# One 512-column product for the upper half of the expert tiles, with index numbers and gates read from PSUM

## The chip, the cores and the metric

The kernel runs on one core of a Trainium2 chip. The metric is the device time of one execution in microseconds. TensorE (PE) multiplies, with PEld as its weight loads; VectorE (DVE), ScalarE (ACT) and GpSimd (POOL) do the elementwise work; SyncE (SP) issues the transfers from HBM. SBUF is the working memory, PSUM holds the products in 8 banks of 512 float32 for each partition.

## The reference

There are two layers over 256 tokens of width 1024: a gated short convolution or an attention mixer, each followed by the same channel mixer, which is where nearly all of the time goes. Its part that matters here, for a normalised input `xc`:

```python
q = (xc @ w_q).reshape(PEER_CHUNK, PEER_HEADS, 2, PEER_HALF)
s1 = jnp.einsum('thd,nd->thn', q[:, :, 0], sub_k1); s2 = jnp.einsum('thd,nd->thn', q[:, :, 1], sub_k2)
v1, i1 = lax.top_k(s1, PEER_TOPK); v2, i2 = lax.top_k(s2, PEER_TOPK)
...
top_s, top_pos = lax.top_k(cand, PEER_TOPK)
e_idx = jnp.take_along_axis(cidx, top_pos, axis=-1)     # 16 of 16384 experts, for 8 heads
g = jax.nn.softmax(top_s, axis=-1)
a = jax.nn.gelu(jnp.einsum('td,thkd->thk', xc, u_emb[e_idx]), approximate=False)
return jnp.einsum('thk,thkd->td', g * a, v_emb[e_idx])
```

## The kernel before

The kernel gathers nothing. It multiplies the input with all 16,384 rows of `peer_u`, takes the Gelu of every product, multiplies that by a dense matrix of gates that is zero except at the chosen experts, and multiplies the result with all rows of `peer_v`. Both matrices come in 128 tiles of 128 experts for each layer: the U tiles (k = 0 to 127), then the V tiles. The products of U tile k stand in `A[:, k]`, experts in partitions and 256 tokens in columns; `A` lies in the buffer `big`.

float32 numbers are split into two float32r parts, high and low, and each product is three products: high times high, high times low, low times high. x^T stands split in `XH` and `XL`, 8 blocks of 256 columns each.

The work on one U tile goes through the engines like this, with three buffers at each stage:

- SP loads the tile into `raw` (L135). DVE transposes it to `tr` (L156). ACT copies the high part to `hi` (L170). POOL subtracts to get the low part `lo`, in two halves (L175). The last four U tiles and all V tiles have their `lo` from DVE.
- PE runs `products`: for each of 8 blocks, hi times XH (L875) and hi times XL (L876), then lo times XH for 8 blocks (L879). These are 24 matmuls of 256 columns, each with its own weight load, into half a PSUM bank. Two tiles share a bank of `lo4` (banks 0 to 3).
- After an odd tile ACT takes the Gelu of the full bank into `big` (L1011).

`next_item` is called once for each tile in program order. It emits the transpose for the tile three ahead and the split for the tile two ahead, then the tile's own products, then side work from a queue: `run_side(budget)` hands out entries as long as a credit lasts, and this order is what stands in each engine's program.

The side work of U tiles 0 to 63 is the top-k search. From U tile 64 on (`gate=U0 + 64`) it is `g_side`: for 32 groups of 8 tokens it builds the dense gates of half of the experts. For a group s, `hots` compares the numbers 0 to 63 (`iota_t`) with the group's row and column indices (`eT`) into one-hot rows in `xbuf` (DVE, L1024, 1536 elements of fp16), `gated` multiplies one part of them by the gates `gT2` (DVE, L1032, 1024 elements of fp16), PE multiplies the two for each token (16 matmuls of 64 columns, L1039, into banks 4 to 7 in turn), and `mult` multiplies `A` by the result (DVE, L1046). The second half of the experts follows in the same way beside V tiles 0 to about 58, with the banks 0 to 3; V accumulates in the other four (L483, 12 matmuls of 512 columns a tile).

Before the U tiles come the queries: `q_out` copies a query product out of PSUM, one token half on ACT (L889), the other on DVE (L890); `q_turn` has PE transpose both (L897). Between the layers, at the end of attention, `close` scales a half of the heads' outputs (DVE, L787), `fin` transposes two of their blocks and splits them (L795, L798, L799), and the output projection follows (L490 to L492).

At the end of the U tiles, `u_last` multiplies the last one; after its fourth block the side queue is emptied and `wsplit(0)` splits the first four blocks of `A` into the space of `XH` and `XL` (ACT L1066, DVE L1067) for the V tiles.

## Time and profile before

| | |
|---|---|
| median of 3 runs | 1839.16 us (1838.45 to 1839.89) |
| the profiled execution | 1836.42 us, with a span of 1834.3 us from first to last instruction |
| PE matmul busy | 1808.1 us, 99% of the span |
| DVE, ACT, POOL busy | 1340.5, 859.6, 790.5 us |
| read from HBM | 315.83 MB, 174 GB/s over the span |
| granted TensorE clock | 0.999 of full speed |

The busy time of PE is modelled for pipelined matmuls: each lasts 0.28 to 0.40 us by its row, and the next one starts before it ends. So the distance between starts is read here, not the duration. U tiles 64 to 127 of layer 0 run from 334 to 537 us of the span, those of layer 1 from 1257 to 1460 us.

### The profile page before, as it was taken

How to read it: one execution, taken by the hardware profiler on the slowest of the kernel's cores; microseconds unless marked ns; L12 is line 12 of the kernel's file. 1: busy time of each engine (PE TensorE's matmuls, PEld its weight loads, DVE VectorE, ACT ScalarE, POOL GpSimd, SP SyncE). 2: the span in 40 equal slices, each digit the busy share in tenths (PEclk: the TensorE clock that was granted, in tenths of full speed). 3: DMA queues.
4: the chain of work that ended last, by engine and by line, in shares of the span. 5: the costliest groups of instructions: out<-in, count | busy, mean ns of one | idle time of the engine just before them, and what ended most of it. 6: DMA issues, size and time to landing. Idle time of an engine off the chain costs nothing.

```text
span 1834.3 us, 34269 instructions
## 1 busy us (share of the span) xinstructions
PE 1808.1 (99%) x13009; PEld 1627.4 (89%) x13009; DVE 1340.5 (73%) x2115; ACT 859.6 (47%) x1041; POOL 790.5 (43%) x549
## 2 busy tenths in 40 slices
PE   9999999999999999999999999999999999999998
PEld 8979999999998888888788799999999988888886
DVE  4748888688778887555567587887788788875555
ACT  5455455444444444444454554555443444445443
POOL 1047899999940000000200378999999500000000
PEclk9999999999999999999999999999999999999999
DMA  6566655555555555666562565555555455556554
GB/s 210 159 197 180 183 158 172 175 170 162 167 167 173 169 177 178 226 194 194 164 185 80 179 198 171 164 165 179 167 166 166 155 181 173 173 176 227 194 194 138
DMA packets 204587, 321.26 MB, mean 175 GB/s; under 512 B 26221, under 2 KB 157317, under 8 KB 203910
## 3 DMA queue, kind: packets, MB, share of 16 engines
q1 hardware_dynamic: 202006, 312.33, 54.8%
q10 hardware_dynamic: 2416, 6.75, 1.1%
q8 instruction: 101, 1.65, 0.4%
q14 instruction: 64, 0.52, 0.1%
HBM read 315.83 MB, written 3.15 MB: 174 GB/s over the span
## 4 chain that ended last, share of the span: by engine, by line
PE 88%; DVE 4%; ACT 2%; DMA 2%; POOL 2%; issue 2%; SPq 0%; DVEq 0%; POOLq 0%; ACTq 0%
PE psum L483 40%; PE psum L875 12%; PE psum L879 12%; PE psum L876 12%; PE psum L1039 3%; PE psum L470 3%; POOL lo L175 2%; DVE big L214 1%; PE psum L516 1%; ACT hi L170 1%; DVE tr L156 1%; DVE lo L175 1%; DMA raw<-in_peer_u_dram 1%; PE psum L903 1%; PE psum L490 0%
## 5 line engine op out<-in xcount | busy, mean ns | idle before, releaser
L175 POOL TENSOR_TENSOR lo<-tr,hi 128x512 fp32r<-128x512 f32 x496 | 732.1, 1513 | 51.5 <-ACT hi L170 49.0
L175 DVE TENSOR_TENSOR lo<-raw,hi 128x1024 fp32r<-128x1024 f32 x316 | 388.2, 1229 | 257.9 <-ACT hi L170 249.3
L170 ACT ACTIVATE hi<-raw 128x1024 fp32r<-128x1024 f32 x331 | 350.1, 1060 | 450.6 <-PE psum L483 375.6
L875 PE MATMUL psum<-xh,hi 128*128 128x256 f32 x2032 | 505.2, 287 | 1.1 <-ACT hi L170 1.1
L876 PE MATMUL psum<-xl,hi 128*128 128x256 f32 x2032 | 498.4, 283 | 0.0
L483 PE MATMUL psum<-hi,xh 128*128 128x512 f32 x1104 | 435.5, 396 | 0.7 <-ACT hi L170 0.7
L483 PE MATMUL psum<-hi,xl 128*128 128x512 f32 x1104 | 428.9, 390 | 0.0
L156 DVE STREAM_TRANSPOSE tr<-raw 128x1024 f32<-128x1024 f32 x256 | 317.2, 1239 | 133.0 <-POOL lo L175 113.7
L875 PEld LDWEIGHTS psum<-xh,hi 128*128 128x128 f32 x2032 | 389.6, 192 | 1.7 <-ACT hi L170 1.5
L876 PEld LDWEIGHTS psum<-xl,hi 128*128 128x128 f32 x2032 | 390.2, 192 | 0.2
L170 ACT ACTIVATE hi<-tr 128x1024 fp32r<-128x1024 f32 x256 | 270.1, 1057 | 123.2 <-DVE tr L156 85.0
L175 POOL TENSOR_TENSOR lo<-raw,hi 128x512 fp32r<-128x512 f32 (+1 forms) x27 | 49.1, 1843 | 604.8 <-ACT hi L170 535.9
L483 PE MATMUL psum<-lo,xh 128*128 128x512 f32 x1104 | 295.3, 389 | 0.4 <-POOL lo L175 0.4
L879 PE MATMUL psum<-xh,lo 128*128 128x256 f32 x2032 | 288.5, 284 | 6.2 <-POOL lo L175 6.2
L879 PEld LDWEIGHTS psum<-xh,lo 128*128 128x128 f32 x2032 | 263.1, 192 | 8.7 <-POOL lo L175 8.5
L483 PEld LDWEIGHTS psum<-lo,xh 128*128 128x128 f32 x1104 | 207.2, 188 | 43.7 <-POOL lo L175 0.8
L483 PEld LDWEIGHTS psum<-hi,xh 128*128 128x128 f32 x1104 | 207.3, 188 | 41.7 <-ACT hi L170 1.1
L483 PEld LDWEIGHTS psum<-hi,xl 128*128 128x128 f32 x1104 | 207.7, 188 | 40.7
L1011 ACT ACTIVATE big<-psum 128x512 f32<-128x512 f32 x126 | 75.2, 597 | 289.1 <-PE psum L879 289.1
L1138 POOL TENSOR_TENSOR big<-xbuf,big 128x256 f32<-128x256 f32 x2 | 1.4, 732 | 379.8 <-DVE rstd L346 379.8
L1024 DVE TENSOR_TENSOR xbuf<-iota_t,eT 128x1536 f16<-128x1536 f16 x128 | 126.8, 991 | 15.2 <-PE psum L1039 14.9
L1032 DVE TENSOR_TENSOR xbuf<-xbuf,gT 128x1024 f16<-128x1024 f16 x128 | 99.7, 779 | 1.1
(173 smaller groups left out, 1440.0 us busy)
## 6 DMA issues: line engine op xcount, KB each, us to landing
raw<-in_peer_u_dram SPq DMA_DIRECT2D x1024, 128.0 KB, 2.8
raw<-in_peer_v_dram SPq DMA_DIRECT2D x256, 512.0 KB, 3.4
raw<-in_conv_w_in_dram SPq DMA_DIRECT2D x96, 128.0 KB, 2.8
raw<-in_attn_w_qkv_dram SPq DMA_DIRECT2D x96, 128.0 KB, 2.7
raw<-in_peer_w_q_dram SPq DMA_DIRECT2D x64, 128.0 KB, 2.7
raw<-in_conv_w_out_dram SPq DMA_DIRECT2D x8, 512.0 KB, 3.8
raw<-in_attn_w_o_dram SPq DMA_DIRECT2D x8, 512.0 KB, 3.2
x_dram<-xbuf ACTq DMA_DIRECT2D x2, 1024.0 KB, 4.7
```

Source lines behind the costliest of these rows:

```text
L156: dve.transpose(TR[m % 3].rearrange("p b (g i) -> p g b i", g=4), RAW[m % 3].rearrange("p (g m) -> p g m", m=256))
L170: act.activation(HI[m % 3], src, AF.Copy)
L175: eng.tensor_sub(LO[m % 3][:, c], src[:, c], HI[m % 3][:, c])
L470: pe.matmul(banks[c // 2][:, (c % 2) * 256:(c % 2) * 256 + 256], w[:, c * 128:c * 128 + 128], xx[:, b], start=(b == 0 and p == 0 and c % 2 ...
L483: pe.matmul(banks[j], x[:, j // 2 * 128:j // 2 * 128 + 128], w[:, j % 2 * 512:j % 2 * 512 + 512], start=(first and p == 0), stop=(last and ...
L875: pe.matmul(o, hi[:, s], XH[:, b], start=(b == 0), stop=False)
L876: pe.matmul(o, hi[:, s], XL[:, b], start=False, stop=False)
L879: pe.matmul(o, lo[:, s], XH[:, b], start=False, stop=(b == 7))
L1011: act.activation(A[:, k - 1:k + 1].rearrange("p k t -> p (k t)"), bk, AF.Gelu)
L1024: dve.tensor_tensor(HOT[s % 2].rearrange("p b (r k) t -> p b r k t", r=3), iota_t[:, None, None].to_broadcast([128, TOK // 2, 3, 64, 2]), ...
L1032: dve.tensor_tensor(OHG[s % 2], one_hot[:, None].to_broadcast([128, 2, TOK // 2, 64, 2]), gT2[:, s, :, :, None, :].to_broadcast([128, 2, T ...
L1039: pe.matmul(o, pairs[:, t // 2, :, t % 2], OHG[s % 2][:, a, t // 2, :, t % 2], start=(a == 0), stop=(a == 1))
```

## The change

`XH` and `XL` become the two halves of one tile `X2`, 8 blocks of 512 columns. For U tiles from 64 on, hi is multiplied by the whole block: one matmul of 512 columns takes the place of two of 256, and the low part is added to the first 256 columns as before. A tile then fills a bank by itself, and the four banks of `lo4` hold two pairs of tiles. After an odd tile, ACT copies the second halves of both banks to `A`, DVE adds the first halves (`both`, put behind the tile's side work by `state["last"]`), and ACT takes the Gelu in SBUF one pair later.

In `g_side`, `hold` first copies `iota_t` and `gT2` into the fourth bank with two small DVE instructions; `hots` reads the numbers from there and `gated` the gates. The gates' products go around three banks.

`q_out` copies both token halves on ACT. The second `close` stands before the second `fin` and not behind it.

```diff
 WARM = 22
+WIDE = (64, 64)
...
-    XH = sb.tile([128, 8, 256], F32R, name="xh")
-    XL = sb.tile([128, 8, 256], F32R, name="xl")
+    X2 = sb.tile([128, 8, 512], F32R, name="x2")
+    XH, XL = X2[:, :, 0:256], X2[:, :, 256:512]
...
         run_side(budget)
+        state.pop("last", lambda: None)()
...
             if p == 5:
                 close(0)
+            if p == 9:
+                close(1)
             if p >= 8:
                 fin(p - 8)
-        close(1)
...
+        def upper(o, hi, b):
+            w = hi[:, b * 128:b * 128 + 128]
+            if o.shape[-1] == 512:
+                pe.matmul(o, w, X2[:, b], start=(b == 0), stop=False, skip_group_check=True)
+            else:
+                pe.matmul(o, w, XH[:, b], start=(b == 0), stop=False)
+                pe.matmul(o, w, XL[:, b], start=False, stop=False)
+        def lower(o, lo, b):
+            pe.matmul(o[:, 0:256], lo[:, b * 128:b * 128 + 128], XH[:, b], start=False, stop=(b == 7),
+                      skip_group_check=(o.shape[-1] == 512))
         def products(o, hi, lo):
             for b in range(8):
-                s = slice(b * 128, b * 128 + 128)
-                pe.matmul(o, hi[:, s], XH[:, b], start=(b == 0), stop=False)
-                pe.matmul(o, hi[:, s], XL[:, b], start=False, stop=False)
+                upper(o, hi, b)
             for b in range(8):
-                s = slice(b * 128, b * 128 + 128)
-                pe.matmul(o, lo[:, s], XH[:, b], start=False, stop=(b == 7))
+                lower(o, lo, b)
...
         def q_out(g):
-            act.activation(qs[:, 0], head_bank(g, 0), AF.Copy)
-            dve.tensor_copy(qs[:, 1], head_bank(g, 1))
+            for t in range(2):
+                act.activation(qs[:, t], head_bank(g, t), AF.Copy)
...
+        def u_bank(k):
+            return lo4[k % 4] if k >= WIDE[l] else lo4[(k // 2) % 4][:, (k % 2) * 256:(k % 2) * 256 + 256]
+        def gelu(k):
+            a = A[:, k - 1:k + 1].rearrange("p k t -> p (k t)")
+            act.activation(a, a if k >= WIDE[l] else lo4[(k // 2) % 4], AF.Gelu)
+        def halves(k, s):
+            return psum[:, k // 2 % 2 * 1024:k // 2 % 2 * 1024 + 1024].rearrange("p (k s t) -> p k s t", k=2, s=2)[:, :, s]
+        def both(k):
+            a = A[:, k - 1:k + 1]
+            dve.tensor_tensor(a, halves(k, 0), a, op=OP.add)
+        def u_done(k):
+            assert k < 95 or st["listed"]
+            if k < WIDE[l]:
+                gelu(k)
+                return
+            if k - 2 > WIDE[l]:
+                gelu(k - 2)
+            act.activation(A[:, k - 1:k + 1], halves(k, 1), AF.Copy)
+            state["last"] = lambda: both(k)
         def u_mm(k):
             def f(hi, lo):
-                bk = lo4[(k // 2) % 4]
-                o = bk[:, (k % 2) * 256:(k % 2) * 256 + 256]
-                products(o, hi, lo)
+                products(u_bank(k), hi, lo)
                 if k % 2:
-                    assert k < 95 or st["listed"]
-                    act.activation(A[:, k - 1:k + 1].rearrange("p k t -> p (k t)"), bk, AF.Gelu)
+                    u_done(k)
...
+            held = banks[3].bitcast(F16)
+            numbers = held[:, 0:128].rearrange("p (k t) -> p k t", t=2)
+            gate_rows = held[:, 128:640].rearrange("p (s a b t) -> p s a b t", a=2, b=TOK // 2, t=2)
+            def hold():
+                words = banks[3].bitcast(U32)
+                for o, src in ((0, iota_t.rearrange("p k t -> p (k t)")), (64, gT2.rearrange("p s a b t -> p (s a b t)"))):
+                    w = src.bitcast(U32)
+                    dve.tensor_scalar(words[:, o:o + w.shape[-1]], w, 0, None, op0=OP.logical_shift_right)
...
                 dve.tensor_tensor(HOT[s % 2].rearrange("p b (r k) t -> p b r k t", r=3),
-                                  iota_t[:, None, None].to_broadcast([128, TOK // 2, 3, 64, 2]),
+                                  numbers[:, None, None].to_broadcast([128, TOK // 2, 3, 64, 2]),
                                   eT[hf][:, s, :, :, None, :].to_broadcast([128, TOK // 2, 3, 64, 2]),
...
                 dve.tensor_tensor(OHG[s % 2], one_hot[:, None].to_broadcast([128, 2, TOK // 2, 64, 2]),
-                                  gT2[:, s, :, :, None, :].to_broadcast([128, 2, TOK // 2, 64, 2]), op=OP.mult)
+                                  gate_rows[:, s, :, :, None, :].to_broadcast([128, 2, TOK // 2, 64, 2]), op=OP.mult)
...
-                        o = banks[s % 4][:, t * 64:t * 64 + 64]
+                        o = banks[s % 3][:, t * 64:t * 64 + 64]
...
-                dve.scalar_tensor_tensor(w, banks[s % 4].rearrange("p (t k) -> p k t", k=64), 1.0 / GSC, w,
+                dve.scalar_tensor_tensor(w, banks[s % 3].rearrange("p (t k) -> p k t", k=64), 1.0 / GSC, w,
...
+            add(0.5, hold, gate=gate)
...
         def u_last(hi, lo):
-            bk = lo4[(NK // 2 - 1) % 4]
+            o = u_bank(NK - 1)
             for b in range(8):
-                s = slice(b * 128, b * 128 + 128)
-                pe.matmul(bk[:, 256:512], hi[:, s], XH[:, b], start=(b == 0), stop=False)
-                pe.matmul(bk[:, 256:512], hi[:, s], XL[:, b], start=False, stop=False)
-                pe.matmul(bk[:, 256:512], lo[:, s], XH[:, b], start=False, stop=(b == 7))
+                upper(o, hi, b)
+                lower(o, lo, b)
                 if b == 3:
                     drain_side(second)
                     wsplit(0)
-            act.activation(A[:, NK - 2:NK].rearrange("p k t -> p (k t)"), bk, AF.Gelu)
+            u_done(NK - 1)
+            state.pop("last")()
+            gelu(NK - 1)
```

On PE, in the program where the gates' matmuls of a group end and the next upper U tile begins, stood before (psum is the bank, xh and xl the parts of x^T; L875 and L876 stand there eight times in turn for a tile):

```order
L1039 MATMUL psum<-xbuf 128x64
L875 MATMUL psum<-xh,hi_73 128x256
L876 MATMUL psum<-xl,hi_73 128x256
...
L879 MATMUL psum<-xh,lo_76 128x256 x8
L875 MATMUL psum<-xh,hi_74 128x256
L876 MATMUL psum<-xl,hi_74 128x256
```

and now, with x_78 for `X2`:

```order
L1085 MATMUL psum<-xbuf 128x64
L878 MATMUL psum<-x_78,hi_74 128x512 x8
L884 MATMUL psum<-x_78,lo_77 128x256 x8
L878 MATMUL psum<-x_78,hi_72 128x512 x8
L884 MATMUL psum<-x_78,lo_75 128x256 x8
```

Eight rows of 512 columns stand where sixteen of 256 stood; the low products are the same eight.

On DVE, in the middle of the upper U tiles, stood before (L156 transposes a coming tile; L1024, L1032 and L1046 are `hots`, `gated` and `mult`):

```order
L156 STREAM_TRANSPOSE tr_70<-raw_67 128x4x8x32
L1024 TENSOR_TENSOR xbuf<-iota_t,eT_84 128x1536
L156 STREAM_TRANSPOSE tr_71<-raw_68 128x4x8x32
L1032 TENSOR_TENSOR xbuf<-xbuf,gT_86 128x1024
L1046 SCALAR_TENSOR_TENSOR big<-psum,big 128x64x8
L156 STREAM_TRANSPOSE tr_69<-raw_66 128x4x8x32
```

and now (L157, L1070, L1078 and L1092 are the same four, L1030 is `both`):

```order
L157 STREAM_TRANSPOSE tr_69<-raw_66 128x4x8x32
L1070 TENSOR_TENSOR xbuf<-psum,eT_83 128x1536
L1030 TENSOR_TENSOR big<-psum,big 128x512
L157 STREAM_TRANSPOSE tr_70<-raw_67 128x4x8x32
L1078 TENSOR_TENSOR xbuf<-xbuf,psum 128x1024
L1092 SCALAR_TENSOR_TENSOR big<-psum,big 128x64x8
```

Each of the two large fp16 instructions now has one operand in PSUM, and one addition stands there for each pair of tiles. On ACT the pair's row `L1011` of before (Gelu out of PSUM) has become two, the Gelu in SBUF of the pair before and the copy out of PSUM. The orders on POOL and SP are the same as before.

## Rows read from the trace of the kernel before

**Rows 1.** The page: the span, and PE's busy time, share and instructions.
```profile
span 1834.3 us, 34269 instructions
PE 1808.1 (99%) x13009; PEld 1627.4 (89%) x13009; DVE 1340.5 (73%) x2115; ACT 859.6 (47%) x1041; POOL 790.5 (43%) x549
```

**Rows 2.** Busy time of each engine in two stretches of 50 us, with the granted clock, the DMA share and GB/s: upper U tiles, and V tiles beside the second half of the gates.
```profile
400.00:450.00 50.00, 50.00 (x521) 49.61 (x520) 39.12 (x43) 20.75 (x24) 50.00 (x33) 1.00 0.55 165
...
600.00:650.00 50.00, 50.00 (x356) 40.69 (x356) 43.52 (x49) 21.13 (x21) 0.00 (x0) 1.00 0.52 175
```

**Rows 3.** PE in order of time from the end of a tile, over the 16 matmuls of a gate group, to the end of the next tile's high products; columns are start, duration, engine, line, operation, tiles, shape, count.
```profile
406.46 0.64 PE L879 MATMUL psum<-xh,lo 128*128 128x256 f32 x4
406.94 0.65 PE L1039 MATMUL psum<-xbuf 128*128 128x64 f16 x16
407.43 0.36 PE L875 MATMUL psum<-xh,hi 128*128 128x256 f32 x1
407.63 0.28 PE L876 MATMUL psum<-xl,hi 128*128 128x256 f32 x1
...
409.31 0.28 PE L876 MATMUL psum<-xl,hi 128*128 128x256 f32 x1
```

**Rows 4.** PE in order of time in the late V tiles, where no gates run: the first matmuls of two successive tiles, 12 matmuls apart.
```profile
800.73 0.39 PE L483 MATMUL psum<-hi,xh 128*128 128x512 f32 x1
...
803.45 0.39 PE L483 MATMUL psum<-hi,xh 128*128 128x512 f32 x1
```

**Rows 5.** PE in order of time: the first matmul of U tile 64 and of U tile 126 in layer 0.
```profile
334.47 0.28 PE L875 MATMUL psum<-xh,hi 128*128 128x256 f32 x1
...
531.16 0.28 PE L875 MATMUL psum<-xh,hi 128*128 128x256 f32 x1
```

**Rows 6.** POOL by line, first from 150 to 250 us (lower U tiles), then from 350 to 500 us (upper U tiles): count, busy us, mean ns, idle before it.
```profile
L175 POOL TENSOR_TENSOR lo<-tr,hi 128x512 fp32r<-128x512 f32 x66 | 83.9, 1303 | 17.5 <-ACT hi L170 17.5
L175 POOL TENSOR_TENSOR lo<-tr,hi 128x512 fp32r<-128x512 f32 x95 | 151.6, 1635 | 0.0
```

**Rows 7.** PE's gate matmuls and DVE by line from 350 to 500 us (upper U tiles), then DVE from 560 to 690 us (V tiles, POOL idle).
```profile
L1039 PE MATMUL psum<-xbuf 128*128 128x64 f16 x419 | 17.2, 193 | 0.0
L156 DVE STREAM_TRANSPOSE tr<-raw 128x1024 f32<-128x1024 f32 x47 | 58.4, 1242 | 29.5 <-POOL lo L175 29.5
L1024 DVE TENSOR_TENSOR xbuf<-iota_t,eT 128x1536 f16<-128x1536 f16 x26 | 26.7, 1025 | 0.3 <-PE psum L1039 0.2
L1032 DVE TENSOR_TENSOR xbuf<-xbuf,gT 128x1024 f16<-128x1024 f16 x26 | 24.0, 924 | 0.2
L1046 DVE SCALAR_TENSOR_TENSOR big<-psum,big 128x512 f32<-128x512 f32 x27 | 18.1, 670 | 0.0
...
L1024 DVE TENSOR_TENSOR xbuf<-iota_t,eT 128x1536 f16<-128x1536 f16 x24 | 22.9, 952 | 5.1 <-PE psum L1039 5.1
L1032 DVE TENSOR_TENSOR xbuf<-xbuf,gT 128x1024 f16<-128x1024 f16 x24 | 16.5, 686 | 0.2
```

**Rows 8.** DVE and POOL in order of time in the upper U tiles: one POOL subtraction beside `mult` and one beside `hots`, with a transpose between.
```profile
413.23 0.65 DVE L1046 SCALAR_TENSOR_TENSOR big<-psum,big 128x512 f32<-128x512 f32 x1
413.26 1.29 POOL L175 TENSOR_TENSOR lo<-tr,hi 128x512 fp32r<-128x512 f32 x1
414.59 1.25 DVE L156 STREAM_TRANSPOSE tr<-raw 128x1024 f32<-128x1024 f32 x1 [0.71 <-POOL lo L175]
415.75 2.07 POOL L175 TENSOR_TENSOR lo<-tr,hi 128x512 fp32r<-128x512 f32 x1
415.76 0.92 DVE L1024 TENSOR_TENSOR xbuf<-iota_t,eT 128x1536 f16<-128x1536 f16 x1
```

**Rows 9.** Prices, from the groups by line and shape over the whole span: a float32 DVE instruction of 1024 elements; one of 512 elements out of SBUF, and one with an operand out of PSUM; an ACT instruction of 512 elements from SBUF, and one from PSUM.
```profile
L175 DVE TENSOR_TENSOR lo<-raw,hi 128x1024 fp32r<-128x1024 f32 x316 | 388.2, 1229 | 257.9 <-ACT hi L170 249.3 <-DMA raw<-in_peer_w_q_dram 3.1 <-DMA raw<-in_attn_w_qkv_dram 3.0
...
L214 DVE TENSOR_TENSOR big<-big 128x512 f32<-128x512 f32 x8 | 5.5, 690 | 0.2
L214 DVE TENSOR_TENSOR big<-psum,big 128x512 f32<-128x512 f32 x8 | 5.5, 682 | 0.0
...
L332 ACT ACTIVATE big<-big 128x512 f32<-128x512 f32 x4 | 2.5, 630 | 2.7 <-DMA big<-in_x_dram 2.7
L1011 ACT ACTIVATE big<-psum 128x512 f32<-128x512 f32 x126 | 75.2, 597 | 289.1 <-PE psum L879 289.1
```

**Rows 10.** The query transposes in order of time: the first set of layer 0 with ACT's copy, the second set of layer 0, and the second set of layer 1; in brackets the idle time before and what ended it.
```profile
126.27 0.60 ACT L889 ACTIVATE big<-psum 128x512 f32<-128x512 f32 x1
126.98 1.04 PE L897 MATMUL psum<-ident,big 128*128 128x128 f32 x8
...
140.61 0.98 PE L897 MATMUL psum<-ident,big 128*128 128x128 f32 x7 [2.29 <-DVE big L890]
...
1063.79 0.98 PE L897 MATMUL psum<-ident,big 128*128 128x128 f32 x7 [1.32 <-DVE big L890]
```

**Rows 11.** The end of attention in order of time: the output projection waits for the second `close`.
```profile
1008.66 1.28 DVE L787 TENSOR_TENSOR big<-psum,big 128x512 f32<-128x512 f32 x2
1009.40 0.50 PE L490 MATMUL psum<-hi,xh 128*128 128x512 f32 x1 [0.63 <-DVE big L787]
```

**Rows 12.** The start of the V tiles in order of time: the split of `A` that they wait for, and the first matmul that reads its low part.
```profile
536.77 1.23 DVE L1067 TENSOR_TENSOR xl<-big,xh 128x1024 fp32r<-128x1024 f32 x1 [1.17 <-ACT xh L1066]
538.76 0.62 PE L483 MATMUL psum<-hi,xl 128*128 128x512 f32 x2
```

More of the change, by code (lines that the diff above doesn't have):

```diff
@@ L1064, in wsplit @@
         def wsplit(m):
-            a = A[:, 4 * m:4 * m + 4].rearrange("p k t -> p (k t)")
-            act.activation(WH[m % 2].rearrange("p k t -> p (k t)"), a, AF.Copy)
-            dve.tensor_sub(WL[m % 2].rearrange("p k t -> p (k t)"), a, WH[m % 2].rearrange("p k t -> p (k t)"))
+            a = A[:, 4 * m:4 * m + 4]
+            act.activation(WH[m % 2], a, AF.Copy)
+            dve.tensor_sub(WL[m % 2], a, WH[m % 2])
         def u_last(hi, lo):
-            bk = lo4[(NK // 2 - 1) % 4]
+            o = u_bank(NK - 1)
             for b in range(8):
-                s = slice(b * 128, b * 128 + 128)
-                pe.matmul(bk[:, 256:512], hi[:, s], XH[:, b], start=(b == 0), stop=False)
-                pe.matmul(bk[:, 256:512], hi[:, s], XL[:, b], start=False, stop=False)
-                pe.matmul(bk[:, 256:512], lo[:, s], XH[:, b], start=False, stop=(b == 7))
+                upper(o, hi, b)
+                lower(o, lo, b)
                 if b == 3:
```

## The prediction

> **What bounds the kernel now.** The page comes first: PE is busy for 99% of the span [rows 1], so time can only come from PE having less to do or waiting less. The change works on the upper U tiles, so the second view is the busy time of each engine there: PE and POOL both show 50.00 of 50 us, DVE 39.12, ACT 20.75, at a full granted clock [rows 2]. Two engines at the limit at once is what the reader is to see: relieving one alone would leave the other.
>
> PE's rows in order of time tell what its 99% consist of. After a gate group the high products of 256 columns start 0.120 us apart: 14 steps from 407.63 to 409.31 [rows 3]. Where the matmuls have 512 columns, in the late V tiles, 12 of them take 803.45 - 800.73 = 2.72 us, so 0.2267 us each [rows 4]. Two narrow matmuls cost 0.240 us, a wide one with as many columns 0.2267: about 0.013 us are paid for each matmul beside its columns. A gate group costs more than its 0.03 us a matmul: the low products reach 406.46 + 3 x 0.12 = 406.82, and the second high product starts at 407.63, 0.81 us later in place of 0.24, so 0.57 us a group [rows 3]. From 350 to 500 us there are 419 / 16 = 26.2 groups [rows 7].
>
> An upper tile lasts (531.16 - 334.47) / 62 = 3.172 us [rows 5]. Hence 150 us hold 47.3 tiles, 0.55 groups a tile, and the sum 24 x 0.120 + 0.55 x 0.57 = 3.19 us is the whole period: PE is dense there and waits for nobody.
>
> POOL is the other limit. Its subtraction takes 1.303 us beside the top-k work, with idle time, and 1.635 us in the upper tiles, with none [rows 6]. Two for each tile make 3.27 us, a little less where rows overlap, so POOL just keeps up with 3.172. Why it is slower is seen in order of time: beside `mult`, which reads one operand from PSUM, the subtraction takes 1.29 us; beside `hots`, which reads both from SBUF, 2.07 [rows 8]. DVE feels it too: `hots` and `gated` average 1.025 and 0.924 us there, and 0.952 and 0.686 where POOL is idle, and the transposes waited 29.5 us for POOL [rows 7].
>
> **The change part by part.**
>
> *The wide product.* In each tile from 64 to 127, sixteen matmuls of 0.120 us become eight of 512 columns. The trace has no such product with `hi` as weights, but it has the same shape and type with one weight load each [rows 4]. Bounds: no gain if two halves' price stays, 0.240; 0.2267 as in V. I take 0.2267, the nearest row. 8 x (0.240 - 0.2267) = 0.107 us a tile, so the period becomes 3.065 us; 64 tiles, two layers: **-13.7 us**.
>
> *POOL must follow.* If `hots` and `gated` no longer hold it up, a tile needs 2 x 1.303 = 2.61 us of POOL, under 3.065. With today's 1.635 it could not go below about today's 3.172 (bound: the whole 13.7 lost). I take the first: `mult` has exactly the form that the two get, one operand in PSUM and one in SBUF, and costs POOL nothing [rows 8].
>
> *DVE must follow.* For a pair of tiles: two transposes of 1.242, 1.1 groups of 0.952 + 0.686 + 0.670, and the new addition, 0.682 by a row of the same shape [rows 7, 9]: 2.48 + 2.54 + 0.68 = 5.70 us of 2 x 3.065 = 6.13. Successive DVE instructions overlap by 0.08 us (414.59 + 1.25 against 415.76 [rows 8]), about 0.5 us a pair, so some 5.2. This supposes that the two fp16 instructions keep their pace, about 0.6 us for 1000 elements, with an operand in PSUM, which no row shows. Bounds: unchanged, or one element at a time as in float32, where 1024 elements take 1.229 and 512 take 0.690 [rows 9]; then 1.23 for `gated` and 1.229 + 0.539 = 1.77 for `hots`. I take unchanged: in float32 an operand in PSUM costs nothing against SBUF (0.682 against 0.690 for 512 elements [rows 9]), so the place alone is no reason to slow down.
>
> The Trainium skill speaks against this: VectorE: DVE Perf Modes, section The perf-mode tier table, gives `tensor_tensor` double speed for bf16 in SBUF and single speed for any operand in PSUM, though the same section's paragraph on PSUM operands still allows a mode of two elements a cycle. No run here shows either; by the table the time would be that of the single-speed rival below.
>
> *The added ACT work.* For a pair, a copy out of PSUM of 0.597 and a Gelu in SBUF of 0.630 stand for one Gelu of 0.597 [rows 9]: +0.63 us on an engine with 20.75 of 50 us busy [rows 2]. Hidden.
>
> *The new wait.* `both` waits for ACT's copy, which waits for PE's end of the odd tile; behind it on DVE stand the transposes and side work of the next pair. It can begin some 0.75 us after that end and is over at 1.4, and the next transpose at 2.7. That transpose belongs to the tile that PE starts three tiles, 9.2 us, later, with ACT's 1.06 and POOL's 2.6 us between: over 2 us to spare. The bank itself is wanted 6.1 us after that end. Cost 0; if DVE had no slack in a pair, every us over 6.13 would come back 64 times.
>
> *The start of V.* `wsplit(0)` is over at 536.77 + 1.23 = 538.00, its first reader starts at 538.76 [rows 12]. The copy, addition and Gelu of the last pair now stand before later splits on ACT and DVE (about 2 us), but those are needed two V tiles, 5.4 us, later. Cost 0; without that cover up to 2 us a layer.
>
> *`q_out`.* PE's second set of transposes waited 2.29 and 1.32 us for a DVE copy that stood behind top-k work [rows 10]. ACT is free by then: -3.6 us. In the first set of layer 0 both copies now follow on ACT from 126.27, the second ending near 127.4, while PE arrives at 126.98: up to +0.4. Together **-3.2 us**.
>
> *`close`.* The output projection waited 0.63 us for DVE [rows 11]; with the scaling first it starts some 0.7 us earlier and is done in time: **-0.7 us**, and no other work waits for the subtraction that it now precedes within 4 us.
>
> *Small things.* `hold` adds two short DVE instructions four times in all. Three gate banks in place of four bring no wait, since `mult` of group s - 3 stands ahead of `gated` of s in DVE's own order. POOL and SP keep their order.
>
> Sum: -13.7 - 3.2 - 0.7 = -17.6 us, made against the profiled 1836.42 us, which gives 1818.8. That execution lies 2.7 us under the median, so from 1839.16 the forecast is **1821.6 us**.
>
> **The rivals.**
>
> *DVE becomes the bound (slower).* If fp16 with a PSUM operand runs one element at a time, a pair of upper tiles costs DVE 2.48 + 1.1 x (1.77 + 1.23 + 0.67) + 0.68 = 7.2 us, with the overlaps 6.7: 3.35 us a tile, +0.18 on 128 tiles = +23. The first V tiles have a period of 12 x 0.2267 + 0.55 x 0.57 = 3.03 us, and DVE would need 1.229 + 0.307 (a quarter of the split of `A`, 1.23 [rows 12]) + 0.55 x 3.67 = 3.55, with overlaps 3.33: +0.30 on 2 x 58 tiles = +35. With -3.9 from the rest: about 1893 us, up to 1950 without overlaps. It decides from where a group of `hots` and `gated` takes 0.8 us more than its 1.64. For it: no row has the form, and the skill's table. Against it: the float32 rows.
>
> *POOL stays the bound (hardly faster).* If POOL is held up by any DVE instruction on SBUF, an upper tile stays at 3.172 and only 3.9 us are won: 1835.3. For it: POOL has no idle time now. Against it: the 1.29 beside `mult` and 1.303 in the lower tiles, beside as many transposes.
>
> *PE waits a little at the pair ends (less fast).* DVE's slack in a pair is 0.4 to 0.9 us, and side work comes in lumps. If one pair in three cost 0.3 us, 64 pairs would give back 6: 1828.
>
> **How the numbers follow.** The forecast 0.75, with its own range of 1817 to 1826; pair ends 0.06 (1828); POOL 0.06 (1835); DVE 0.13 (1893). A difference under 0.2%, 3.7 us, cannot be told from none here. Faster: 0.75 + 0.06 + half of POOL's, 0.84; same 0.03; slower 0.13. The range that leaves out no more than 2 in 10 runs from 1816 to 1836, up to the POOL case; it leaves out DVE's.
>
> **What would show it.** Right: 512-column matmuls 0.227 us apart in the upper U tiles, tiles there 3.06 us apart; POOL's subtraction at about 1.30 us with idle time again; `hots` and `gated` at 0.95 and 0.69 us; no idle PE before the second query transposes and in the output projection. Wrong: `hots` near 1.8 us and PE waiting for the gates' rows; POOL still at 1.6 us; PE waiting for `both` at the start of an even tile; or wide matmuls 0.24 us apart.

## The result, and the profile after

The changed kernel takes **1821.97 us** (median of 4 runs, 1821.39 to 1822.77) against 1838.81 us (4 runs, 1835.63 to 1839.89): a ratio of 0.9915, 95% interval 0.9901 to 0.9928. The forecast was 1821.6, its range 1816 to 1836. The profiled execution of the changed kernel took 1822.49 us, its span is 1820.7.

From the page of the changed kernel, as [rows 1]: busy time, share of the span, instructions.
```profile
PE 1797.7 (99%) x11985; PEld 1573.6 (86%) x11985; DVE 1353.9 (74%) x2183; ACT 894.6 (49%) x1109; POOL 710.7 (39%) x549
```
PE has 1024 matmuls fewer and is still the full engine. DVE and ACT have 68 instructions more each, and POOL the same 549 in 80 us less.

The first stretch of [rows 2], upper U tiles, in the changed kernel: length, busy time by engine, granted clock, DMA share, GB/s.
```profile
400.00:450.00 50.00, 50.00 (x390) 44.18 (x389) 42.16 (x52) 25.02 (x32) 41.14 (x33) 1.00 0.61 173
```
In the upper U tiles POOL went from 50.00 to 41.14 us: only PE is at its limit now. The clock is full as before.

PE of the changed kernel in order of time over two tiles, the last of them followed by a gate group (as [rows 3]: start, duration, line, operation, tiles, shape, count):
```profile
404.63 2.09 PE L878 MATMUL psum<-x,hi 128*128 128x512 f32 x8
406.56 1.11 PE L884 MATMUL psum<-x,lo 128*128 128x256 f32 x8
407.51 2.00 PE L878 MATMUL psum<-x,hi 128*128 128x512 f32 x8
409.35 1.11 PE L884 MATMUL psum<-x,lo 128*128 128x256 f32 x8
410.31 0.65 PE L1085 MATMUL psum<-xbuf 128*128 128x64 f16 x16
...
333.59 0.40 PE L878 MATMUL psum<-x,hi 128*128 128x512 f32 x1
...
525.13 0.40 PE L878 MATMUL psum<-x,hi 128*128 128x512 f32 x1
```
Eight wide products without a gate group ahead take 409.35 - 407.51 = 1.84 us, 0.230 each: less than the 0.240 of two narrow ones, and not the 0.2267 of the V tiles in [rows 4]. The last two rows, the starts of tiles 64 and 126, answer to [rows 5]: (525.13 - 333.59) / 62 = 3.089 us a tile where 3.172 stood.

POOL and DVE by line from 350 to 500 us, then DVE from 560 to 690 us (as [rows 6, 7]: count, busy us, mean ns, idle before it and what ended it):
```profile
L176 POOL TENSOR_TENSOR lo<-tr,hi 128x512 fp32r<-128x512 f32 x98 | 123.8, 1293 | 27.7 <-ACT hi L171 27.7
L157 DVE STREAM_TRANSPOSE tr<-raw 128x1024 f32<-128x1024 f32 x49 | 60.3, 1231 | 0.0
L1070 DVE TENSOR_TENSOR xbuf<-psum,eT 128x1536 f16<-128x1536 f16 x26 | 23.9, 921 | 0.9 <-PE psum L1085 0.9
L1078 DVE TENSOR_TENSOR xbuf<-xbuf,psum 128x1024 f16<-128x1024 f16 x27 | 17.8, 659 | 0.2
L1092 DVE SCALAR_TENSOR_TENSOR big<-psum,big 128x512 f32<-128x512 f32 x26 | 17.5, 672 | 0.0
L1030 DVE TENSOR_TENSOR big<-psum,big 128x512 f32<-128x512 f32 x24 | 16.6, 692 | 22.7 <-ACT big L1040 22.7
...
L1070 DVE TENSOR_TENSOR xbuf<-psum,eT 128x1536 f16<-128x1536 f16 x25 | 23.8, 952 | 4.0 <-PE psum L1085 4.0
...
L1078 DVE TENSOR_TENSOR xbuf<-xbuf,psum 128x1024 f16<-128x1024 f16 x24 | 16.4, 683 | 0.3
```
The subtraction fell from 1635 to 1293 ns and POOL now waits for its input, 27.7 us in 150. `hots` (L1070) and `gated` (L1078) cost 921 and 659 ns with an operand in PSUM. Beside V tiles they cost 952 and 683, as before from SBUF alone (952 and 686). The means of before in the upper tiles, 1025 and 924, hide two kinds of rows: of 26 `gated`, 19 behind a transpose took 0.648 us, as they do now, and 7 right behind `hots` took 1.67 (now 0.689). One of each, in the kernel before:
```profile
358.87 0.65 DVE L1032 TENSOR_TENSOR xbuf<-xbuf,gT 128x1024 f16<-128x1024 f16 x1
...
416.71 1.67 DVE L1032 TENSOR_TENSOR xbuf<-xbuf,gT 128x1024 f16<-128x1024 f16 x1
```
The second starts while the subtraction of 2.07 us in [rows 8] still runs, from 415.75 to 417.82. So a `gated` that comes in the middle of a subtraction takes longer; where the two start together, as `hots` and the subtraction in [rows 8], it is POOL's row that does. DVE's 29.5 us of waiting for POOL are gone; instead it waits 22.7 us for ACT's copy ahead of the new addition.

Who waits for whom in the upper U tiles (330 to 525 us: us in all, times, longest):
```profile
ACT big L1040 <- PE psum L884: 61.4, 30, 2.7
ACT hi L171 <- DVE tr L157: 32.0, 30, 1.8
POOL lo L176 <- ACT hi L171: 31.3, 29, 1.7
DVE big L1030 <- ACT big L1040: 28.4, 29, 1.6
```
Everybody waits along the chain that PE leads, and PE waits for nobody. DVE's wait ahead of the addition, 28.4 us in 29 waits, is 0.98 us each, one wait a pair of tiles.

The query transposes (as [rows 10]): the first and the second set of layer 0, and the second set of layer 1.
```profile
128.56 0.33 PE L910 MATMUL psum<-ident,big 128*128 128x128 f32 x1
129.05 0.98 PE L910 MATMUL psum<-ident,big 128*128 128x128 f32 x7 [0.16 <-ACT big L903]
...
139.94 1.03 PE L910 MATMUL psum<-ident,big 128*128 128x128 f32 x8
...
1055.41 1.03 PE L910 MATMUL psum<-ident,big 128*128 128x128 f32 x8
```
The waits of 2.29 and 1.32 us for DVE are gone; a short one for ACT's second copy has come in the first set, where the prediction looked for it.

By stage, from the start of U tile 0, of tile 64 and the last U product of each layer (us, profiled executions):
```
                      before            after        difference
start to U tile 0     135.17            137.07         +1.90
tiles 0-63            199.30, 197.97    196.52, 196.43  -4.32
tiles 64-127          202.33, 202.33    197.04, 197.05 -10.57
V0 to U tile 0 of L1  522.52            521.91          -0.61
V1 to the end         374.72            374.69          -0.03
```
The first row is no effect of the change but for the short wait just shown: it lay between 135.2 and 138.1 us in all kernels here, whatever they change behind it. Without it the stages give -15.5 us, and the medians -16.8. The fourth row is not safe either, as the run with `q_out` and `close` alone shows below.

### The profile page after: what moved, and what is told of

Its sections match the earlier page's. It is cut to its first block, busy times and chain, and to the rows that moved or that the text cites. A ratio compares the mean times of both kernels' runs of the same rounds, so it can differ in the third digit from the quotient of the medians.

```text
span 1820.7 us, 32357 instructions
## 1 busy us (share of the span) xinstructions
PE 1797.7 (99%) x11985; PEld 1573.6 (86%) x11985; DVE 1353.9 (74%) x2183; ACT 894.6 (49%) x1109; POOL 710.7 (39%) x549
## 3 DMA queue, kind: packets, MB, share of 16 engines
q8 instruction: 94, 1.54, 0.4%
## 4 chain that ended last, share of the span: by engine, by line
PE 90%; DVE 4%; DMA 2%; ACT 1%; POOL 1%; issue 1%; SPq 0%; DVEq 0%; ACTq 0%; POOLq 0%
PE psum L485 41%; PE psum L878 13%; PE psum L884 12%; PE psum L880 5%; PE psum L881 5%; PE psum L1085 3%; PE psum L472 3%; PE psum L518 2%; DVE big L215 1%; POOL lo L176 1%; DVE tr L157 1%; PE psum L916 1%; DVE lo L176 1%; DMA raw<-in_conv_w_out_dram 1%; ACT hi L171 1%
## 5 line engine op out<-in xcount | busy, mean ns | idle before, releaser
L485 PE MATMUL psum<-hi,x 128*128 128x512 f32 x2208 | 553.0, 392 | 0.7 <-ACT hi L171 0.7
L485 PEld LDWEIGHTS psum<-hi,x 128*128 128x128 f32 x2208 | 409.0, 188 | 82.6 <-ACT hi L171 1.1
L157 DVE STREAM_TRANSPOSE tr<-raw 128x1024 f32<-128x1024 f32 x256 | 316.0, 1234 | 64.2 <-POOL lo L176 38.2
L884 PE MATMUL psum<-x,lo 128*128 128x256 f32 x2048 | 292.0, 283 | 6.2 <-POOL lo L176 6.2
L485 PE MATMUL psum<-lo,x 128*128 128x512 f32 x1104 | 295.2, 389 | 0.4 <-POOL lo L176 0.4
L884 PEld LDWEIGHTS psum<-x,lo 128*128 128x128 f32 x2048 | 273.6, 191 | 18.6 <-POOL lo L176 8.6
L878 PE MATMUL psum<-x,hi 128*128 128x512 f32 x1024 | 263.6, 398 | 0.0
L880 PE MATMUL psum<-x,hi 128*128 128x256 f32 x1024 | 252.7, 284 | 0.8 <-ACT hi L171 0.8
L881 PE MATMUL psum<-x,hi 128*128 128x256 f32 x1024 | 251.1, 283 | 0.0
L485 PEld LDWEIGHTS psum<-lo,x 128*128 128x128 f32 x1104 | 207.1, 188 | 43.9 <-POOL lo L176 0.8
L878 PEld LDWEIGHTS psum<-x,hi 128*128 128x128 f32 x1024 | 183.6, 189 | 33.3
L880 PEld LDWEIGHTS psum<-x,hi 128*128 128x128 f32 x1024 | 196.3, 192 | 1.5 <-ACT hi L171 1.2
L881 PEld LDWEIGHTS psum<-x,hi 128*128 128x128 f32 x1024 | 196.4, 192 | 0.2
L1070 DVE TENSOR_TENSOR xbuf<-psum,eT 128x1536 f16<-128x1536 f16 x128 | 119.9, 937 | 10.1 <-PE psum L1085 10.1
```

What stands on the lines that cost most here:

```text
L157: dve.transpose(TR[m % 3].rearrange("p b (g i) -> p g b i", g=4), RAW[m % 3].rearrange("p (g m) -> p g m", m=256))
L485: pe.matmul(banks[j], x[:, j // 2 * 128:j // 2 * 128 + 128], w[:, j % 2 * 512:j % 2 * 512 + 512], start=(first and p == 0), stop=(last and ...
L878: pe.matmul(o, w, X2[:, b], start=(b == 0), stop=False, skip_group_check=True)
L880: pe.matmul(o, w, XH[:, b], start=(b == 0), stop=False)
L881: pe.matmul(o, w, XL[:, b], start=False, stop=False)
L884: pe.matmul(o[:, 0:256], lo[:, b * 128:b * 128 + 128], XH[:, b], start=False, stop=(b == 7), skip_group_check=(o.shape[-1] == 512))
```

## The experiments

**Four kernels that make a square.** All four have the early `close` and the `q_out` on ACT. They differ in the product (narrow or wide) and in where the numbers and gates lie (SBUF or PSUM); the changed kernel is the fourth corner.

The change without the wide product (e1):
```diff
-WIDE = (64, 64)
+WIDE = (128, 128)
@@ u_last
-            state.pop("last")()
-            gelu(NK - 1)
```


> Everything of the change but the wide product: all U tiles keep two matmuls of 256 columns, numbers and gates are read from PSUM, q_out is on ACT, close is earlier. Theory (PE's matmul count sets the upper tiles, POOL's relief only makes room): an upper tile stays at 3.17 us with PE dense, POOL's subtraction falls to 1.30 us and POOL has idle time; only the 4.9 us of q_out and close are won, about 1834 us. Rival (POOL was the real limit of the upper tiles, so its relief alone brings the gain): an upper tile at 3.09 us, about 1823 us.

Measured: 1833.31 us (1831.15 to 1834.25), ratio 0.9972 (0.9961 to 0.9984), 3.1725 us for an upper tile. POOL and `hots` from 350 to 500 us:
```profile
L176 POOL TENSOR_TENSOR lo<-tr,hi 128x512 fp32r<-128x512 f32 x95 | 120.2, 1296 | 30.3 <-ACT hi L171 30.3
...
L1070 DVE TENSOR_TENSOR xbuf<-psum,eT 128x1536 f16<-128x1536 f16 x26 | 24.8, 954 | 36.0 <-PE psum L1085 35.9
```
POOL is relieved just as in the changed kernel, and the tile is as long as before: PE was the bound, and the relief alone buys nothing.

The change with numbers and gates left in SBUF (e2):
```diff
@@ hots, gated
-                                  numbers[:, None, None].to_broadcast([128, TOK // 2, 3, 64, 2]),
+                                  iota_t[:, None, None].to_broadcast([128, TOK // 2, 3, 64, 2]),
-                                  gate_rows[:, s, :, :, None, :].to_broadcast(...), op=OP.mult)
+                                  gT2[:, s, :, :, None, :].to_broadcast(...), op=OP.mult)
-            add(0.5, hold, gate=gate)
```


> The change with numbers and gates read from SBUF as before (no hold), the wide product kept. Theory (POOL becomes the limit at 1.6 us a subtraction): an upper tile stays near 3.17 us, POOL has no idle time and PE waits for lo; about 1832 us. Rival (POOL's long rows are only slack that it fills, and it follows when PE is faster): 3.09 us a tile, about 1822 us.

Measured: 1827.41 us (1826.46 to 1828.17), ratio 0.9944 (0.9927 to 0.9961), 3.131 us for an upper tile. That lies between the two expectations. From 350 to 500 us:
```profile
L176 POOL TENSOR_TENSOR lo<-tr,hi 128x512 fp32r<-128x512 f32 x96 | 151.7, 1621 | 0.0
...
L1070 DVE TENSOR_TENSOR xbuf<-iota_t,eT 128x1536 f16<-128x1536 f16 x25 | 31.0, 1240 | 0.0
L1078 DVE TENSOR_TENSOR xbuf<-xbuf,gT 128x1024 f16<-128x1024 f16 x26 | 30.2, 1162 | 0.2
```
POOL is the bound: no idle time, 1.62 us for each subtraction. PE is as fast as in the changed kernel until it waits for the second half of a low part, in some of the tiles 75 to 121, as here in tile 95:
```profile
431.78 0.73 PE L884 MATMUL psum<-x,lo 128*128 128x256 f32 x4 [0.23 <-POOL lo L176]
```
These longer steps between low products add up to 2.6 us a layer, which is the whole difference to the changed kernel's upper tiles. Two subtractions with the overlap of successive rows fit into 3.131 us, so POOL had some 0.04 us a tile to spare in the kernel before, though its rows show no idle time there, and half of the wide product's gain fits in. `hots` and `gated` pay too: 1240 and 1162 ns instead of 921 and 659.

The kernel before with `q_out` and `close` alone (e3):
```diff
+            if p == 9:
+                close(1)
@@
-        close(1)
@@ q_out
-            act.activation(qs[:, 0], head_bank(g, 0), AF.Copy)
-            dve.tensor_copy(qs[:, 1], head_bank(g, 1))
+            for t in range(2):
+                act.activation(qs[:, t], head_bank(g, t), AF.Copy)
```


> The kernel before with q_out on ACT and the earlier close alone. Theory (the stage times of the two profiles add up): U tiles 0 to 63 of the two layers 2.8 and 1.5 us shorter, the stage from layer 0's last U tile to layer 1's first 0.6 us shorter, upper tiles at 3.17: 4.9 us less than before, about 1834 us. Rival (what PE gains at the queries is waited for again at the end of the top-k work): no lower-U gain, 0.6 us alone, about 1838 us.

Measured: 1832.33 us (1831.18 to 1833.8), ratio 0.9968 (0.9956 to 0.9979). Tiles 0 to 63 last 196.56 and 196.45 us, as in the changed kernel. Upper tiles stay at 3.1725. The stretch between the layers is 522.43 us, 0.1 less than before where 0.6 were expected. The wait of [rows 11] is gone, but 15 us later in the same projection PE now waits for a low part, whose weights ACT in turn waits 2.9 us for:
```profile
1022.45 0.50 PE L492 MATMUL psum<-lo,xh 128*128 128x512 f32 x1 [0.52 <-DVE lo L175]
```
Of the kernels with the early `close`, four (this one, and three of those below) have this wait and 522.4 to 522.6 us. Six, the changed kernel among them, do not have it and take 521.6 to 521.9. The one with three additions (e8) does not have it either; it takes 522.83, and two starts of PE stand 1.1 us apart at the start of V.

The square, medians in us (the changed kernel was timed beside a before of 1838.81, the others of 1838.62):
```
                  SBUF       PSUM
narrow product    1832.33    1833.31
wide product      1827.41    1821.97
```
The wide product gives 4.9 us with POOL at its limit and 11.3 without; the move to PSUM gives nothing (1 us the wrong way, within the runs' scatter) with the narrow product and 5.4 with the wide one. By the upper tiles of the traces alone, where the start of the run plays no part, it is 5.4 and 10.6, and 0.0 and 5.2. Each part is worth its price only beside the other.

**DVE's slack.** The addition of the pair's halves made twice (e7, below), and three times (e8):
```diff
@@ both
-            dve.tensor_tensor(a, halves(k, 0), a, op=OP.add)
+            for i in range(2):
+                dve.tensor_tensor(a, halves(k, 0), a, op=OP.add)
```


> The changed kernel with the addition of a pair's halves made twice (upper tiles of both layers; the outputs then differ from the reference's). Theory (DVE has slack: in the changed kernel it waits some 0.9 us of the 6.18 us of a pair for the addition's input, and PE does not wait for it): one addition more of 0.69 us is hidden: within 4 us of 1822. Rival (the addition stands in the chain that frees a bank for TensorE, so that its length is paid): 63 pairs x 0.69 = 43 us more, 1865.

> The same with the addition made three times (the outputs then differ from the reference's). Theory (the slack is 0.9 us a pair and no more): 1.38 - 0.9 = 0.5 us a pair, 63 pairs: 30 us more, 1852 (1840 to 1865), TensorE waiting for DVE in every pair. Rival (paid in full): 87 us more, 1909. Rival (hidden still): 1822.

Measured: 1822.01 us (1821.38 to 1823.17) with two, 3.089 us a tile, so the second is free. DVE's wait ahead of the addition fell from 28.4 to 9.2 us, by 0.64 a pair:
```profile
DVE big L1031 <- ACT big L1041: 9.2, 20, 1.6
```
With three, 1843.36 us (1842.72 to 1845.21), 3.233 us a tile. From 400 to 450 us DVE is full and PE no longer:
```profile
400.00:450.00 50.00, 48.88 (x378) 42.55 (x377) 49.42 (x63) 23.29 (x31) 38.06 (x31) 1.00 0.55 159
```
The upper stage grew by 9.4 us a layer, 0.30 us a pair, where two additions of 0.69 came on top. So the slack is 1.08 us a pair, a little more than the 0.4 to 0.9 of the prediction, and the loss smaller than expected for that reason.

**The wide product everywhere (e4).**
```diff
-WIDE = (64, 64)
+WIDE = (0, 0)
```


> The change with the wide product from U tile 0 on. Theory (a tile saves 0.083 us wherever PE is dense): 64 more tiles a layer, up to 10.6 us less than the changed kernel, 1811 us, less what PE waits longer for DVE and POOL at the end of the top-k work. Rival (DVE's top-k work leaves no room for one more addition of 0.69 us in each pair: 41 of 50 us are busy there, and 6 come on top): the waits there grow by as much as is saved, 1820 to 1830 us.

Measured: 1827.41 us (1825.12 to 1828.74), 5.4 more than the changed kernel, and within the rival's range. Tiles 0 to 63 take 198.01 us instead of 196.5, so the stages show 3.1 of the 5.4. By tile 41 the wide tiles have gained 3.3 us in each layer, and by tile 48 all of it is lost. Up to 260 us PE has no wait there; then it has many. Two of them, in order of time:
```profile
264.04 0.74 PE L884 MATMUL psum<-x,lo 128*128 128x256 f32 x4 [1.51 <-POOL lo L176]
...
277.25 2.09 PE L878 MATMUL psum<-x,hi 128*128 128x512 f32 x8 [2.46 <-DVE big L1030]
```
DVE has top-k work in these tiles, and it is what feeds POOL and frees the banks. The same addition that is hidden in the upper tiles is not hidden here: the second row waits for it.

**Why a wide product costs 0.230 and not 0.2267.** In the changed kernel's trace the time from one start to the next depends on the place in the run. Means over the upper tiles from 350 to 500 us, ns:
```
8 wide behind 8 narrow (22 tiles)       233  236  228  232  231  227  227  227
8 wide behind a gate group (26 tiles)   314  231  236  228  233  231  227  227
8 narrow behind 8 wide (49 tiles)       113  119  120  120  120  120  120  120
```
Only the sixth wide one has the pace of the V tiles (0.2267), and the first narrow one is short. Behind a gate group the same sequence comes one place later (the expectation below takes the two kinds of tiles together and names the seventh). The wide ones' means are the same to 2 ns in the kernel with POOL at its limit (e2), which speaks against the other engines as the cause. The experiment puts the two kinds in turn (e5):
```diff
@@ products
+            if o.shape[-1] == 512:
+                for b in range(8):
+                    upper(o, hi, b)
+                    lower(o, lo, b)
+                return
```


> The changed kernel, with the 8 wide and 8 narrow products of an upper tile in turn (block by block) instead of 8 wide and then 8 narrow. In the changed kernel's trace a wide product right behind a narrow one takes 0.233 us to the next start and only the seventh 0.2267, and the first narrow one behind a wide one takes 0.113 instead of 0.120. Theory (the excess belongs to the passage from narrow to wide, and is given back at the passage from wide to narrow): a pair of 0.233 + 0.113 = 0.346, a tile 8 x 0.346 + 0.293 for its share of gate groups = 3.063 instead of 3.089, 126 tiles x 0.026 = 3.3 us less: about 1818.7. Rival A (each return to wide products costs its own 0.030 us, nothing comes back): 8 x (0.233 + 0.120) + 0.293 = 3.117, 3.5 us more: 1825.5. Rival B (the excess belongs to the time within the tile, by what other engines do then): period as it is, 1822. Beside these: the low part must now stand ready when the tile begins, 1.84 us earlier than before; where POOL is late for that, TensorE shows gaps before a tile's first narrow product, and the time rises by them; spacings within a tile still tell the three apart.

Measured: 1820.86 us (1820.06 to 1822.1), ratio 0.9908 (0.9892 to 0.9925), which by itself is not to be told from the changed kernel. The stage tells it: the upper tiles take 196.31 us in both layers, 0.73 less each, 0.012 a tile, where the changed kernel and all its variants of the lower tiles and of DVE's slack, but the one that overran it, agree within 0.01. PE in order of time:
```profile
407.43 0.40 PE L878 MATMUL psum<-x,hi 128*128 128x512 f32 x1
407.66 0.28 PE L884 MATMUL psum<-x,lo 128*128 128x256 f32 x1
407.78 0.39 PE L878 MATMUL psum<-x,hi 128*128 128x512 f32 x1
...
408.81 0.40 PE L878 MATMUL psum<-x,hi 128*128 128x512 f32 x1
```
Four couples, a wide and a narrow product each, take 408.81 - 407.43 = 1.38 us, 0.346 a couple, the theory's figure and that of 0.2267 + 0.120: what a wide product costs more behind a narrow one, the next narrow one gives back. In runs of eight behind narrow ones, the eight wide ones lose 0.027 us and the narrow ones give back 0.008. Rivals A and B fall. The theory had 0.026 a tile and 0.012 came: the mean couple over the stretch is 0.3474, and the gate group now takes 0.496 us instead of 0.487. Why the pace settles only after five products is not shown.

**Where the wide product pays below tile 64.** The first edit (e6); `u_bank`, `gelu` and `u_done` then ask `wide(k)`:
```diff
+EARLY = (32, 32)
@@
+        def wide(k):
+            return k < EARLY[l] or k >= WIDE[l]
```


> The changed kernel with tiles 0 to 31 of both layers wide as well (32 to 63 narrow, 64 to 127 wide). With all tiles wide the kernel lost, by gaps of TensorE between tiles 40 and 57, where DVE's top-k work fills it. Theory (the wide product pays wherever DVE has 0.35 us a tile to spare, and DVE was busy 19 of 25 us there in the changed kernel): tiles 1 to 31 gain 0.09 us each, 2 x 31 x 0.09 = 5.6 us, and the stretch of tiles 32 to 63 keeps its time: 1816 to 1818. Rival (the top-k work is one chain on DVE with an end that the tiles wait for: what the early tiles gain is given back as longer gaps at tiles 40 to 57): 1821 to 1824, with more idle TensorE there than the 5 us or so of the changed kernel.

Measured: 1819.59 us (1818.5 to 1821.04), ratio 0.9898 (0.9881 to 0.9915). Tiles 0 to 63 take 195.16 and 195.11 us, 1.3 less a layer, half of the 2.8 expected. Most of the other half stands in a new row in tile 41 (the expectations below call it tile 40), which the changed kernel does not have:
```profile
263.46 0.75 PE L885 MATMUL psum<-x,lo 128*128 128x256 f32 x4 [1.07 <-POOL lo L177]
```
PE's starts stand 1.35 us apart there. So both expectations hold in part: the early tiles gain, and PE gives half of it back before the end of the top-k work. Then both edits together, with 32 (e9) and with 16 (e10) early tiles (only `EARLY` differs):

> Tiles 0 to 31 and 64 to 127 wide, and in every wide tile the wide and narrow products in turn. Theory (the two edits are independent: the order gave 0.73 us a layer in the upper tiles, the early wide tiles 1.36 and 1.32 us a layer): 2 x (0.73 + 1.34) + 2 x 31 x 0.012 = 4.9 us of the stages less than the changed kernel, about 1817. Rival (in turn, a tile needs its low part at its start, and in the early tiles DVE, which feeds POOL, was busy 18 to 20 us in 20, so the low part comes late): gaps of TensorE within tiles 0 to 31 eat the gain there, 1819 to 1822.

> The same with only tiles 0 to 15 wide of the lower half. In e6 the early wide tiles gained 2.7 us a layer and one new gap of TensorE of 1.35 us at tile 40 gave half of it back. Theory (the gap comes from DVE's work that the additions of tiles 16 to 31 pushed towards tile 40; without these it goes): tiles 1 to 15 gain 0.097 us each, 2 x 15 x 0.097 = 2.9, and the order 1.46: 4.4 us less than the changed kernel, 1817 to 1818, and no gap of over 0.5 us in tiles 32 to 41. Rival (the gap stands there anyway once the early tiles are shorter): it gives back 2 x 1.3 us, 1820.

Measured: 1818.85 us (1817.98 to 1819.97), ratio 0.9892 (0.9875 to 0.9908), with 32; **1818.06 us** (1816.84 to 1819.35), ratio 0.9889 (0.9873 to 0.9906), with 16, against 1837.88 of before on that chip. The U stage of a layer is 2.07 and 1.97 us shorter than in the changed kernel with 32 early tiles, where 2.4 were expected for the edits added up, and 2.25 and 2.21 with 16, as expected. The wait in tile 41 stands in the first and not in the second, whose first wait in these tiles is in tile 42,
```profile
265.41 0.74 PE L885 MATMUL psum<-x,lo 128*128 128x256 f32 x4 [0.81 <-POOL lo L177]
```
which the changed kernel has too. The theory's reason, work that the additions of tiles 16 to 31 push towards tile 41, is hardly in the traces. These are the rows of POOL that make the second half of that tile's low part, in e6 and in e10:
```profile
260.05 3.35 POOL L177 TENSOR_TENSOR lo<-tr,hi 128x512 fp32r<-128x512 f32 x1
...
258.04 3.37 POOL L177 TENSOR_TENSOR lo<-tr,hi 128x512 fp32r<-128x512 f32 x1
```
Counted from the start of U tile 0 (138.10 and 136.26 us) they end at 125.30 and 125.15 us; in the changed kernel the same row ends at 126.55. The sixteen additions delay the low part by 0.15 us, but with them PE is at tile 41 0.94 us sooner than with sixteen early tiles. So in these two kernels the low part comes 1.25 and 1.40 us earlier than in the changed one, and what PE gains beyond that it waits for. It is no fixed limit: with all tiles wide (e4) the same part ends at 123.39 us, and the large waits come from tile 42 on. What sets it is not shown. Sixteen early tiles give what thirty-two give. The two do not differ by their times, but both are faster than the kernel before, and by the stages than the changed one.

## Why the prediction was right, point by point

*What bounds the kernel.* Right in the main: PE was at its limit and POOL within 0.04 us a tile of it. The square shows it: the relief of POOL alone gives nothing, and the wide product alone half of what both give.

*The wide product, -13.7 us: mis-sized.* It gave -10.6 (upper tiles, both layers). The failed step is the price of 0.2267, taken from V tiles where only wide products follow each other. Behind eight narrow ones the mean is 0.230. By the rows, 8 x (0.240 - 0.230) = 0.08 us a tile; 0.083 came.

*POOL must follow.* Right in the value (1.303 forecast, 1.293 measured). Right in the mechanism: four subtractions in a row beside `gated`, `mult`, a transpose and `hots` keep their pace:
```profile
409.34 5.05 POOL L176 TENSOR_TENSOR lo<-tr,hi 128x512 fp32r<-128x512 f32 x4 [1.11 <-ACT hi L171]
```
5.05 / 4 = 1.26 us each, where one beside `hots` took 2.07 in [rows 8]. The Trainium skill has this rule (SBUF — State Buffer, Who interferes with whom): a DVE instruction with two inputs in SBUF contends with a GpSimd instruction that reads SBUF, one with at most one, outside the modes that use both ports, does not; these rows agree. The bound on the other side, the whole gain lost at 1.635 us, was too dark: the wide product with POOL held up still gained half.

*DVE must follow; the new wait.* Right. `hots` and `gated` lost nothing by the operand in PSUM. The Trainium skill's rule that spoke against it (VectorE: DVE Perf Modes, The perf-mode tier table: single speed for `tensor_tensor` with any operand in PSUM) does not hold for this form, fp16 with one operand in PSUM and one in SBUF: beside V tiles 952 and 683 ns, against 952 and 686 with both in SBUF, and the 1893 us that hung on it did not come. The added copy and addition cost nothing, as the slack of 1.08 us a pair shows; the case of the pair ends did not come either, for the upper tiles have no wait of PE.

*`q_out`, -3.2 us.* It gave -4.3 over tiles 0 to 63 (-2.8 and -1.5), and the run with `q_out` and `close` alone shows the same there. The small loss foreseen in the first set, which lies ahead of tile 0, came too: 129.05 - 128.56 = 0.49 us between two starts, 0.37 more than the pace of 0.12. Together -3.9. The term was small because the waits were taken as PE's idle time, 2.29 and 1.32 [rows 10], in place of the time from start to start, 2.57 and 1.59 us: 2.52 and 1.54 us are won by tile 1. Another 0.25 us is won at tile 50 of layer 0, where two starts stood 1.02 us apart and now stand 0.76.

*`close`, -0.7 us.* Right in the wait, which is gone, and not sure in the gain. The stretch between the layers is 0.6 us shorter here, but four other kernels with the early `close` gave it back at the wait for weights shown under e3, which the sum did not have.

*The start of V.* Cost 0, right: V to the end is unchanged.

The sum came closer than its terms: 3.1 us too much for the product, 0.7 too little for `q_out`; what is left lies in the scatter of the executions, of which the start alone has some us. The mechanism was right, but that the forecast lies 0.4 us from the median is luck.

## What to carry to other kernels

Where two engines are full in the same stretch, price a change to one against the slack of the other: here the shorter product was worth some 5 us alone and some 11 with POOL relieved, and the relief alone nothing. Take the price of a repeated instruction from a place with the same neighbours, not only the same shape. And work that is hidden in one stretch must be priced again in the next: the addition that is free beside gates (1.08 us of slack a pair) costs PE waits beside top-k. There only as much of a gain stayed as the engines that feed PE could follow: 1.3 us a layer of the 2.7 that 32 early tiles save.

## What the runs showed that had not been expected

- The spacing of matmuls depends on what ran before: 512 columns behind 256 start 228 to 236 ns apart and settle to 227 at the sixth; the first 256 behind 512 takes 113 instead of 120. In turn, a couple costs 0.346 to 0.347 us, the sum of the two settled prices.
- The port contention is paid on both sides. With POOL idle `hots` and `gated` took 952 and 686 ns; with POOL full in the kernel before 1025 and 924 [rows 7], where `gated` took 648 behind a transpose and 1672 behind `hots`; in e2, with DVE without a pause either, 1240 and 1162.
- What `hots` and `gated` take depends on the row ahead of them, and not on where the operand lies. Right behind a transpose `hots` takes 919 ns and `gated` 648 in the changed kernel; in the kernel before, out of SBUF, it is 916 (but for one row that POOL held up) and 648. Beside V tiles, behind DVE's subtraction, they take 951 and 681 to 684 in both kernels, and `hots` after a pause 957, which is why e1, where it waits for PE, has a mean of 954.
